# Eleven single-token lists interleaved with the last eleven two-list units of a PEER block

## The chip, the cores and the metric

The kernel runs on one core of a Trainium2 chip. Its engines are named as in the profile: PE (TensorE) multiplies matrices, DVE (VectorE) and ACT (ScalarE) work elementwise, POOL (GpSimd) issues the gathers, SP issues the plain transfers. The metric is the device time of one execution in microseconds; the time of a version is the median of its runs.

## The reference, cut to what matters

The kernel computes one decoder layer for 256 tokens of width 2048: a mixer (attention beside a state-space scan), and then a PEER feed-forward block, in which each token picks 16 experts in each of 8 heads out of 16384. An expert is one row of `expert_down` and one of `expert_up`. The change touches the PEER block alone:

```python
def peer_ffn(hn, w_query, sub_keys, expert_down, expert_up):
    ...                                   # product keys: the best 16 of 256 candidates per token and head
    gates = jax.nn.softmax(best_s, axis=-1)
    def block(args):
        xb, idx, gb = args
        u = expert_down[idx]
        act = jax.nn.gelu(jnp.einsum('thkd,td->thk', u, xb), approximate=False)
        vv = expert_up[idx]
        return jnp.einsum('thk,thkd->td', (gb * act).astype(vv.dtype), vv)
```

## The kernel before, in words

The mixer, the queries and the routing come first. Then the kernel sorts the used experts into lists of up to 128, one expert per partition. A gather fetches the rows of one list, 128 x 2048 floats, by an indirect DMA that POOL issues (`pump`, L1346). 17 further lists belong to experts whose lower products were computed densely and stored in `zd_dram`; they need no lower row.

*Lower products.* There are three kinds of lists. The 20 lists of kind C serve any token. The 44 lists of the two-list units (`unit_t`, L1460) serve only tokens of one half; a unit takes two such lists. In eight steps PE turns pieces of both rows (`tp`, L1475), ACT and DVE split them into a high and a low part (`turned`, L1449), and PE multiplies them by the tokens into `z` (L1488 to L1490); after the last step come GELU on ACT and a turning back (`zT`, L1504). The 30 single-token lists (`unit_d`, L1601) hold experts used by one token each. For such a list the kernel fetches its gates (`d_prep`, L1558), DVE finds in them the token of each expert (`find`, L1569 to L1571), PE turns the resulting one-hot matrix (`otb`, L1576), ACT copies it (`ot`, L1577), and then in four steps PE multiplies it by the tokens of h (`xe`, L1608) and DVE multiplies the gathered row by that with a running sum (L1614). The single-token lists need h turned (`turn_hn`, L1632): 64 transposes, copied by ACT into `hnt` in the buffers b2 and b3.

*Gates.* `gates` (L1240) builds a table of gates for all experts and tokens in the buffers b0 to b3 and stores each half in eight pieces to `g_dram` (`put`, L1262, on SP). `form` (L1688) fetches the gates of a list from `g_dram` (`fetch_gate`, L1431, on POOL) and multiplies them onto its products on DVE (`multiply`). It keeps a pace, a fraction of a list per step (FR).

*Upper products.* `up_load` and `up_go` (L1811, L1871) split a list's upper rows on ACT and DVE and multiply them by the gated products into `out` (L1889). The first 29 upper lists run among the single-token lists; 15 of them need no split. The others follow.

*What sets the order.* All of this is a list of items, each with a load part and a multiply part. `stream` runs them in order and emits the load parts up to LOOKT = 3 (or LOOKD = 2) items ahead. Work in `bg` (gates, turning h, forming) and in `due` advances by a step after each item. A scheduler then places the instructions of each engine, and every engine works through its own in order. The gathers form one queue in the order of `gathers`: one is issued when a slot of the `ring` is free (`release`, L1365). The ring has five slots during the lists C and the first units, four in the buffer `lo` and one in `xa`. When all gates are stored, `more_rows` (L1369) adds four more in b2 and b3 for the next units (up to unit 17, LATE); after them those buffers take the turned h. When the single-token lists begin (`begin`, L1588), the buffer of h becomes four more slots.

Of the kernel before, what the change touches and what calls it, by code (L numbers as in the profile page):

```python
# [18 lines left out]
P = 128  # L19
T = 256  # L20
# [79 lines left out]
TF = 8  # L100
TG = 4
XZ = 8
SBW = 10
SBR = 8
NPG = 2
# [3 lines left out]
FR = (0.27, 0.1, 0.35)  # L109
# [5 lines left out]
LATE = 17  # L115
TD = -8
# [27 lines left out]
def tile_block(ctx: ExitStack, tc: tile.TileContext, xT, w_f, w_v, w_dt, w_o, w_q, sk, dnt, down, up,  # L144
# [1095 lines left out]
    def gates():  # L1240
# [11 lines left out]
        def products(t0, B, A):  # L1252
            gp = ps_at(f"g_{t0}", (P, G2T, NK))
            for k in range(G2T):
                for j in range(2):
                    nc.tensor.matmul(gp[:, k, :], B[:, :, k], A[:, j, :, k], start=(j == 0), stop=(j == 1))  # L1256
            o = t0 % P
            for c in range(4):
                nc.scalar.activation(gbuf[c][:, :, o:o + G2T].rearrange("p i t -> p t i"), gp[:, :, 32 * c:32 * c + 32], AF.Copy)  # L1259
            if o == P - G2T:  # L1260
                h = t0 // P
                def put(c):  # L1262
                    cs = slice(16 * c, 16 * c + 16)
                    nc.sync.dma_start(g_dram[0:NE].rearrange("(i p) t -> p i t", p=P)[:, cs, h * P:(h + 1) * P],
                                        gbuf[c // 2][:, c % 2 * 16:c % 2 * 16 + 16, :])

                gens["put"] = [lambda c=c: put(c) for c in range(8)]
                gens["last"] = h
# [73 lines left out]
    def regions():  # L1342
        lo_t = rot("raws", "lo", 8192)
        ring.extend((lo_t[:, 2048 * k:2048 * (k + 1)], False) for k in range(4))

    def pump(most=99):  # L1346
        while most and pos[0] < len(gathers):
            what, j, late = gathers[pos[0]]
            can = [s_ for s_ in ring if not (late and s_[1])]
            if not can:  # L1350
                return
            ring.remove(can[0])
            where[what, j] = can[0]
            pos[0] += 1
            most -= 1
            with tc.issue_after(marks["pool"]) if what == "down" and "pool" in marks else ExitStack():
                g = nc.gpsimd.indirect_dma_start(out=can[0][0], out_offset=None, in_=down_rows if what == "down" else up_rows,  # L1357
                                                 in_offset=bass.IndirectOffsetOnAxis(ap=idx[:, 0, j:j + 1], axis=0))
            if "form" in gens and not stage[0]:
                marks["pool"] = g.ins  # L1360

    def row(what, j):
        return where[what, j][0]
# [5 lines left out]
    def more_rows():  # L1369
        while not gens.get("last") or gens["put"]:  # L1370
            yield
        yield from rest(SBW)
        for t in ("b2", "b3"):
            v = rot(f"rows_{t}", t, 4096)
            for k in range(2):
                ring.append((v[:, 2048 * k:2048 * (k + 1)], True))
                pump(1)
                yield from rest(SBR)
        gens["rows"] = True
# [41 lines left out]
    def hnt(p):  # L1421
        gated(0)
        return held(f"hnt{p}", f"b{p + 2}", F32R)
# [25 lines left out]
    def turned(tp, name, mark=False):  # L1449
# [6 lines left out]
        if mark and "form" in gens:  # L1456
            marks["act"], marks["dve"] = a, d
        return hi, lo

    def unit_t(k, r):  # L1460
# [20 lines left out]
        def go(hi, lo, s):  # L1481
            if s == 0:
                keep["z"] = ps_ms(f"z{j}")
            z = keep["z"]
# [6 lines left out]
            if s % 2 and last_b.get((k, r)) is not None:  # L1491
                gated(4)
# [4 lines left out]
            if s == 7:  # L1497
# [3 lines left out]
                def back():  # L1501
                    zT = ps_ms(f"zT{j}")
# [19 lines left out]
    def unit_c(r):  # L1522
# [11 lines left out]
        def go(hi, lo, s):  # L1534
            if s == 0 and r == 0:
                part["xa"] = rot("xa2", "xa", 4096)
                ring.append((part["xa"][:, 0:2048], False))
# [20 lines left out]
    def d_prep(n):  # L1558
# [15 lines left out]
        def turn_():  # L1574
            ot = gens["otb"][:, n % 4 * P:(n % 4 + 1) * P] if "otb" in gens else ps_ms(f"ot{n}", (P, P))
# [8 lines left out]
    def xbank():  # L1584
        gens["xb"].append(gens["xb"].pop(0))
        return gens["xb"][-1]

    def begin():  # L1588
# [6 lines left out]
        marks.pop("pool", None)  # L1595
        gens["x3"] = st.tile([P, 1024], F32R, tag="raw", bufs=NRAW, name="x3")
        v = rot("rows_hn", "hn", 8192)
        ring.extend((v[:, 2048 * k:2048 * (k + 1)], False) for k in range(4))
# [33 lines left out]
    def turn_hn():  # L1632
        while any(v[1] for v in where.values()) or pos[0] < late_at:
            yield
        ring[:] = [v for v in ring if not v[1]]
        for p in range(2):
            for tt in range(2):
                for c in range(4):
                    tp = ps_ms(f"hnt{p}{tt}{c}", (P, 512))
# [48 lines left out]
    def form():  # L1688
        while not gens.get("rows"):
            yield  # L1690
# [17 lines left out]
    for _, k, r in cs_:  # L1708
        items.extend(unit_c(r))
        gathers.append(("down", BASE[k] + r, False))  # L1710
    t_mark = len(items)
    for i, (_, k, r) in enumerate(ts_):
# [192 lines left out]
    def finish(tt, dc):  # L1905
# [5 lines left out]
    timed = [((n + 0.5) / len(ds_) + c / 1000, it, ("down", BASE[k] + r, False) if c == 0 else None)  # L1911
             for n, (_, k, r) in enumerate(ds_) for c, it in enumerate(unit_d(k, r))]
    timed += [((n + 1.0) / early + 0.002 * hf, ups[2 * n + hf], ("up", order[n], False) if hf == 0 else None)
# [7 lines left out]
    for n, _ in pieces[2 * early:]:  # L1921
        if n not in seen:
            seen.add(n)
            gathers.append(("up", order[n], False))
# [122 lines left out]
    bg.append(more_rows())  # L2047
# [14 lines left out]
    for n in range(DLOOK):  # L2062
        d_prep(n)
    stream(items, d_mark, d_mark)
# [91 lines left out]
```

## Time and profile before

| | |
|---|---|
| median of 3 runs | 1660.89 us (1660.86 to 1662.54) |
| the profiled execution | 1660.09 us |
| its span, first to last instruction | 1658.2 us |
| PE, DVE, ACT, POOL busy | 96%, 70%, 47%, 32% |
| mean granted clock of PE | 0.992 |
| two-list units, in the trace | 927.5 to 1172.3 us |
| single-token lists with the early upper lists | 1172.3 to 1356.0 us |
| the other upper lists, to the end | 1356.0 to 1658.2 us |

A row of a timeline has the start, the duration, the engine, the line of the kernel, the operation with its tiles, and in brackets how long the engine had been idle and what ended that. A row of a group has its count after x, then the busy time, the mean duration in ns of one, and the idle time before. PE's matmuls overlap, so a PE that is shown busy may still be slow; the number of matmuls in a stretch tells more. A table of stretches gives for each engine the busy time and the number of instructions, then the granted clock, the share of time in which the DMA engines were busy, and the rate.

### The profile page before, as it was taken

What the parts mean: (1) busy time and instruction counts of PE and PEld (TensorE: products, weight loads), DVE (VectorE), ACT (ScalarE), POOL (GpSimd) and SP (SyncE); (2) the same over time, 40 slices, a digit from 0 to 9 for tenths busy, and PEclk for the clock granted to TensorE, in tenths of its full rate; (3) what the DMA queues carried; (4) which work ended last, traced back from release to release, by engine and by line L of the source; (5) the groups of instructions that cost most, each with busy time, mean ns of one, the idle gap of its engine ahead of it and who ended that gap; (6) DMA issues with size and microseconds to landing.
All of it is one profiled execution on the core that took longest, in us unless ns stands there. A gap on an engine that the chain in (4) does not pass through costs nothing. (4 is left out here: it accounts for less than half of the span.)

```text
span 1658.2 us, 27347 instructions
## 1 busy us (share of the span) xinstructions
PE 1589.6 (96%) x10330; PEld 1404.5 (85%) x10331; DVE 1162.9 (70%) x2556; ACT 781.0 (47%) x1374; POOL 525.2 (32%) x499
## 2 busy tenths in 40 slices
PE   6999999999999999999999997999988999999997
PEld 6999979999888888899999996999755458887776
DVE  7776665853597988646646763655887667888886
ACT  5554457753111202335535664676431025667664
POOL 3001101121000000124414412424665655676851
PEclk9999999999999999999999998999999999999999
DMA  6655544667645433443392298745899999998893
GB/s 203 185 168 153 153 153 140 195 214 231 210 142 160 145 97 99 142 154 103 126 332 97 85 335 301 267 146 181 350 411 338 350 386 340 340 343 297 331 324 120
DMA packets 108809, 366.70 MB, mean 221 GB/s; under 512 B 12705, under 2 KB 48801, under 8 KB 82305
## 3 DMA queue, kind: packets, MB, share of 16 engines
q0 software_dynamic: 35504, 229.43, 37.4%
q1 hardware_dynamic: 70304, 134.23, 26.6%
q8 instruction: 83, 1.36, 0.3%
q10 hardware_dynamic: 2864, 1.24, 0.3%
q14 instruction: 54, 0.43, 0.1%
HBM read 337.24 MB, written 27.92 MB: 220 GB/s over the span
## 5 line engine op out<-in xcount | busy, mean ns | idle before, releaser
L1889 PE MATMUL out<-hi_up,p 128*128 128x512 f32 x716 | 193.7, 391 | 1.3 <-ACT hi_up L1822 1.3
L1455 DVE TENSOR_TENSOR t<-tp,t 128x512 fp32r<-128x512 f32 x176 | 120.9, 691 | 92.7 <-ACT t L1454 91.8
L1889 PEld LDWEIGHTS out<-hi_up,p 128*128 128x128 f32 x716 | 133.5, 188 | 31.3 <-ACT hi_up L1822 3.6
L253 PE MATMUL dn<-xt_t,raw_dn 128*128 128x256 f32 x640 | 158.3, 383 | 0.1
L1357 POOL DMA_INDIRECT raws<-in_down,idx x59 | 62.6, 1061 | 292.7 <-DVE colt L1196 161.8
L1432 POOL DMA_INDIRECT raw_small<-g_dram,idx x111 | 118.2, 1065 | 93.3 <-issue 45.0
L1454 ACT ACTIVATE t<-tp 128x512 fp32r<-128x512 f32 x176 | 105.4, 601 | 64.2 <-PE tp L1475 62.4
L253 PEld LDWEIGHTS dn<-xt_t,raw_dn 128*128 128x128 f32 x640 | 115.2, 193 | 11.7 <-issue 0.5
L253 PE MATMUL pq<-hg,raw_pq 128*128 128x256 f32 x512 | 112.9, 379 | 0.0
L253 PEld LDWEIGHTS pq<-hg,raw_pq 128*128 128x128 f32 x512 | 96.3, 190 | 12.6
L1259 ACT ACTIVATE big<-g 128x128 f32<-128x128 f32 x256 | 70.7, 437 | 75.8 <-PE g L1256 75.8
L1248 POOL TENSOR_TENSOR B<-B,gi 128x512 bf16<-128x512 bf16 x64 | 69.7, 1091 | 91.0 <-DVE B L1246 86.4
L1546 PE MATMUL zc<-hnl,c 128*128 128x256 f32 x320 | 95.9, 300 | 0.0
L1822 ACT ACTIVATE hi_up<-raws 128x1024 fp32r<-128x1024 f32 x74 | 76.7, 1057 | 31.8 <-PE out L1889 30.9
L1475 PE MATMUL tp<-ident,raws 128*128 128x128 f32 x464 | 90.4, 274 | 0.0
L1548 PE MATMUL zc<-hnl,c 128*128 128x256 f32 x320 | 89.1, 279 | 0.0
L1547 PE MATMUL zc<-hnl,c 128*128 128x256 f32 x320 | 89.0, 278 | 0.0
L1822 ACT ACTIVATE hi_up<-rows_hn 128x1024 fp32r<-128x1024 f32 x70 | 73.2, 1056 | 29.1 <-PE out L1889 26.2
L1455 DVE TENSOR_TENSOR c<-tc,c 128x512 fp32r<-128x512 f32 x80 | 55.2, 691 | 43.3 <-ACT c L1454 42.9
L1249 DVE TENSOR_TENSOR A<-O,gi 128x1024 f16<-128x1024 bf16 x64 | 47.5, 743 | 51.6 <-PE g L1256 51.3
L1608 PE MATMUL xe<-hnt,ot 128*128 128x512 f32 x240 | 78.3, 453 | 4.3 <-ACT ot L1577 3.4
L1889 PE MATMUL out<-lo_up,p 128*128 128x512 f32 x254 | 77.4, 397 | 4.4 <-DVE lo_up L1823 4.3
(539 smaller groups left out, 4654.4 us busy)
## 6 DMA issues: line engine op xcount, KB each, us to landing
raw_dn<-in_dnt SPq DMA_DIRECT2D x40, 512.0 KB, 3.9
raw_kq<-in_w_f SPq DMA_DIRECT2D x32, 512.0 KB, 3.8
raw_wo<-in_w_o SPq DMA_DIRECT2D x32, 512.0 KB, 4.7
raw_pq<-in_w_q SPq DMA_DIRECT2D x32, 512.0 KB, 3.8
g_dram<-big SPq DMA_DIRECT2D x16, 1024.0 KB, 13.9
raw_xb<-in_w_f SPq DMA_DIRECT2D x22, 512.0 KB, 4.4
raw_v<-in_w_v SPq DMA_DIRECT2D x16, 512.0 KB, 3.6
raw_z<-in_w_f SPq DMA_DIRECT2D x16, 512.0 KB, 4.0
```

The source lines that it names most:

```text
L253: nc.tensor.matmul(acc, raw[:, j * P:(j + 1) * P], mv[:, k * 8 + j, :], start=(k + j == 0), stop=(k * 8 + j == ND - 1))
L1259: nc.scalar.activation(gbuf[c][:, :, o:o + G2T].rearrange("p i t -> p t i"), gp[:, :, 32 * c:32 * c + 32], AF.Copy)
L1432: nc.gpsimd.indirect_dma_start(out=dst, out_offset=None, in_=g_half if w == P else g_dram, in_offset=bass.IndirectOffsetOnAxis(ap=idx[:, 1 ...
L1454: a = nc.scalar.activation(hi, tp, AF.Copy).ins
L1455: d = nc.vector.tensor_tensor(lo, tp, hi.bitcast(F32), op=OP.subtract).ins
L1475: nc.tensor.transpose(tp[:, (2 * dd + i) * P:(2 * dd + i + 1) * P], row("down", j + i)[:, d * P:(d + 1) * P], ident)
L1546: nc.tensor.matmul(z, wh, ah[:, d, :], start=(d == 0), stop=False)
L1547: nc.tensor.matmul(z, wh, al[:, d, :], start=False, stop=False)
L1548: nc.tensor.matmul(z, wl, ah[:, d, :], start=False, stop=(d == ND - 1))
L1608: nc.tensor.matmul(xe, gens[f"ot{n}"], hnt(p)[:, 2048 * k + 512 * c:2048 * k + 512 * (c + 1)], start=(p == 0), stop=(p == 1))
L1822: marks["act"] = nc.scalar.activation(hi, raw, AF.Copy).ins
L1889: nc.tensor.matmul(oa[tt][2 * hf + c], w[:, k * P:(k + 1) * P], mv[:, c * 512:(c + 1) * 512], start=(i == starts[f, tt, hf] and mv is hi a ...
```

## The change

- Eleven of the 30 single-token lists (DN) leave the stage with the early upper lists. The four steps of list n are put between the first four steps of two-list unit 11 + n (DU). Its row is gathered just before the rows of the next unit. Their `xe` uses the two PSUM banks of the tag `at` (named `xt`). The other 19 are spread over the same 29 upper lists.
- h is turned from unit 5 on (HU) instead of in units 16 to 18, and the first four single-token lists are prepared and `form` starts from unit 9 (GU) instead of unit 4. `form` has a pace of 0.2 instead of 0.27 at first.
- b2 and b3 hold the turned h from then on, so the ring keeps its five slots; `more_rows` is gone.
- The pieces of b2 and b3 are stored first of the second half, and the waits on the stores (`gated`) are set anew.
- The first ten plain units come before the buffered ones (TF, before eight). Sixteen instead of eight of the units' lists keep their products outside b0; the additional eight are in a 128 x 1024 tile `zr`, which is copied to b1 when the single-token stage begins.
- The units' `z` and `zT` share a bank, so that one is left for `otb`.

```diff
-TF = 8
-TG = 4
-XZ = 8
-SBW = 10
-SBR = 8
-NPG = 2
+TF = 10
+XZ = 16
+HU = 5
+GU = 9
+DU = 11
+DN = 11
+NPG = 4
...
-FR = (0.27, 0.1, 0.35)
+FR = (0.2, 0.1, 0.35)
...
-                gens["put"] = [lambda c=c: put(c) for c in range(8)]
+                gens["put"] = [lambda c=c: put(c) for c in (4, 5, 6, 7, 0, 1, 2, 3)]
...
-    def more_rows():
-        while not gens.get("last") or gens["put"]:
-            yield
-        yield from rest(SBW)
-        for t in ("b2", "b3"):
...
     def zh(n, w=P):
+        if n < 8:
+            return part["xa"][:, 3072 + P * n:3072 + P * n + w]
         if n < XZ:
-            return part["xa"][:, 3072 + P * n:3072 + P * n + w]
+            return part["zr"][:, P * (n - 8):P * (n - 8) + w]
         n -= XZ
         if n == 0:
-            gated(6)
+            gated(2)
...
     def hnt(p):
-        gated(0)
+        gated(6 - 2 * p)
...
             if s == 0:
-                keep["z"] = ps_ms(f"z{j}")
-            z = keep["z"]
+                if len(zbank) < DU:
+                    zbank.append(ps_ms(f"z{j}", (P, 512)))
+                else:
+                    zbank.append(zbank[-2])
+                keep["z"] = zbank[-1]
+            z = keep["z"][:, 0:T]
...
     def xbank():
+        if "xb" not in gens:
+            gens["xb"] = [ps_at(f"xt{k}", (P, 512)) for k in range(2)]
...
+    dus = [unit_d(k, r) for _, k, r in ds_]
     for i, (_, k, r) in enumerate(ts_):
-        items.extend(unit_t(k, r))
-        gathers += [("down", BASE[k] + r + x, i >= LATE) for x in range(2)]
-    late_at = SPC[LC] + 2 * LATE
+        u_mark.append(len(items))
+        u = unit_t(k, r)
+        n = i - DU
+        if 0 <= n < DN:
+            u = [x for p in zip(u[:4], dus[n]) for x in p] + u[4:]
+        items.extend(u)
+        if 0 <= n - 1 < DN:
+            gathers.append(("down", d_list[n - 1]))
+        gathers += [("down", BASE[k] + r + x) for x in range(2)]
...
-    stream(items, t_mark + 8 * TG)
+    part["zr"] = raw_tile("zr")
+    stream(items, u_mark[HU])
     pg_all = [t[:, T * k:T * (k + 1)] for t in [raw_tile(f"small{k}") for k in range(2)] for k in range(4)]
-    pgs.extend(pg_all[:NPG])
     gens["hnt"] = turn_hn()
-    gens["form"] = form()
-    bg.extend((gens["hnt"], gens["form"]))
-    stream(items, d_mark - 8)
+    bg.append(gens["hnt"])
+    stream(items, u_mark[GU])
     while gens["hnt"] in bg:
         work()
+    pgs.extend(pg_all[:NPG])
+    gens["form"] = form()
+    bg.append(gens["form"])
+    for n in range(DLOOK):
+        after(1 + 3 * n, lambda n=n: d_prep(n))
+    stream(items, d_mark, d_mark)
```

What this does to the order of the instructions shows at three places. The first is on POOL, where the first fetches of gates stand among the gathers of the units' rows (`raws` and `xa` are the ring's slots, `B` the last products of the table of gates). Before:

```order
L1357 DMA raws<-in_down,idx 128x2048 x2
L1248 TENSOR_TENSOR B_10213<-B_10213,gi 128x512
L1357 DMA raws<-in_down,idx 128x2048
L1357 DMA xa_7255<-in_down,idx 128x2048
L1357 DMA raws<-in_down,idx 128x2048 x4
L1432 DMA raw_small_10539<-g_dram,idx 128x128 x2
L1357 DMA xa_7255<-in_down,idx 128x2048
L1357 DMA raws<-in_down,idx 128x2048
```

After:

```order
L1355 DMA raws<-in_down,idx 128x2048 x2
L1248 TENSOR_TENSOR B_10213<-B_10213,gi 128x512
L1355 DMA raws<-in_down,idx 128x2048
L1355 DMA xa_7256<-in_down,idx 128x2048
L1355 DMA raws<-in_down,idx 128x2048 x4
L1355 DMA xa_7256<-in_down,idx 128x2048
L1355 DMA raws<-in_down,idx 128x2048 x4
L1355 DMA xa_7256<-in_down,idx 128x2048
L1355 DMA raws<-in_down,idx 128x2048 x2
L1420 DMA raw_small_10659<-g_dram,idx 128x128 x2
```

The fetches of gates, which read what SP stores to `g_dram`, have moved behind eight more gathers, the rows of four units.

The second place is PE in a late unit, from its second step on (`xt` are the list's products with h, `otb` the turning for a later list). After the change it reads so; before, the rows of `otb` and `xt` were not there:

```order
L1572 MATMUL otb<-ident,raw_small_10659 128x128
L1465 MATMUL tp_2_12693<-ident,raws 128x128 x4
L1609 MATMUL xt_11482<-hnt_10681,ot_12118 128x512
L1609 MATMUL xt_11482<-hnt_10850,ot_12118 128x512
L1482 MATMUL z_11248<-t_1_12671,hnl 128x256
...
L1498 MATMUL z_11388<-ident,zt_12680 128x128 x2
L1465 MATMUL tp_3_12715<-ident,raws 128x128 x4
L1609 MATMUL xt_11483<-hnt_10681,ot_12118 128x512
L1609 MATMUL xt_11483<-hnt_10850,ot_12118 128x512
```

Eight matmuls of 128x512 and a transpose of each list now stand between the unit's steps, on two banks in turn.

The third place is DVE in such a unit (`t` are the units' low parts, the rows of L1615 the list's four products):

```order
L1443 TENSOR_TENSOR t_0_12213<-tp_0_12208,t_0_12213 128x512
L1615 SCALAR_TENSOR_TENSOR raws,dsc<-raws,xt_11482 128x512
L1443 TENSOR_TENSOR t_1_12237<-tp_1_12232,t_1_12237 128x512
L1680 TENSOR_TENSOR zc<-zc,raw_small_10659 128x256
L1615 SCALAR_TENSOR_TENSOR raws,dsc<-raws,xt_11483 128x512
L1615 SCALAR_TENSOR_TENSOR raws,dsc<-raws,xt_11482 128x512
L1443 TENSOR_TENSOR t_2_12267<-tp_2_12262,t_2_12267 128x512
L1615 SCALAR_TENSOR_TENSOR raws,dsc<-raws,xt_11483 128x512
L1443 TENSOR_TENSOR t_3_12288<-tp_3_12283,t_3_12288 128x512
```

The four products stand among the first four low parts; a low part waits on DVE behind a product that waits for the list's row or for PE.

More of the change, by code (lines that the diff above doesn't have):

```diff
@@ L114 @@
 NA = 4
-LATE = 17
-TD = -8
+TD = -3
 HY = 1
@@ L1343, in regions @@
         lo_t = rot("raws", "lo", 8192)
-        ring.extend((lo_t[:, 2048 * k:2048 * (k + 1)], False) for k in range(4))
+        ring.extend(lo_t[:, 2048 * k:2048 * (k + 1)] for k in range(4))
     def pump(most=99):
         while most and pos[0] < len(gathers):
-            what, j, late = gathers[pos[0]]
-            can = [s_ for s_ in ring if not (late and s_[1])]
-            if not can:
+            what, j = gathers[pos[0]]
+            if not ring:
                 return
-            ring.remove(can[0])
-            where[what, j] = can[0]
+            where[what, j] = ring.pop(0)
             pos[0] += 1
@@ L1356, in pump @@
             with tc.issue_after(marks["pool"]) if what == "down" and "pool" in marks else ExitStack():
-                g = nc.gpsimd.indirect_dma_start(out=can[0][0], out_offset=None, in_=down_rows if what == "down" else up_rows,
+                g = nc.gpsimd.indirect_dma_start(out=where[what, j], out_offset=None, in_=down_rows if what == "down" else up_rows,
                                                  in_offset=bass.IndirectOffsetOnAxis(ap=idx[:, 0, j:j + 1], axis=0))
-            if "form" in gens and not stage[0]:
+            if "hnt" in gens and not stage[0]:
                 marks["pool"] = g.ins
     def row(what, j):
-        return where[what, j][0]
+        return where[what, j]
     def release(what, j):
@@ L1455, in turned @@
         d = nc.vector.tensor_tensor(lo, tp, hi.bitcast(F32), op=OP.subtract).ins
-        if mark and "form" in gens:
+        if mark and "hnt" in gens:
             marks["act"], marks["dve"] = a, d
         return hi, lo
+    zbank = []
     def unit_t(k, r):
@@ L1536, in go @@
                 part["xa"] = rot("xa2", "xa", 4096)
-                ring.append((part["xa"][:, 0:2048], False))
+                ring.append(part["xa"][:, 0:2048])
                 pump()
@@ L1574, in turn_ @@
         def turn_():
-            ot = gens["otb"][:, n % 4 * P:(n % 4 + 1) * P] if "otb" in gens else ps_ms(f"ot{n}", (P, P))
+            if "otb" not in gens:
+                gens["otb"] = ps_ms("otb", (P, 512))
+            ot = gens["otb"][:, n % 4 * P:(n % 4 + 1) * P]
             nc.tensor.transpose(ot, pg[:, P:T], ident)
@@ L1595, in begin @@
         marks.pop("pool", None)
+        kept = held("zh2", "b1")[:, 3072:4096]
+        nc.scalar.activation(kept, part["zr"], AF.Copy)
+        part["zr"] = kept
         gens["x3"] = st.tile([P, 1024], F32R, tag="raw", bufs=NRAW, name="x3")
         v = rot("rows_hn", "hn", 8192)
-        ring.extend((v[:, 2048 * k:2048 * (k + 1)], False) for k in range(4))
+        ring.extend(v[:, 2048 * k:2048 * (k + 1)] for k in range(4))
         pump()
@@ L1688, in form @@
     def form():
-        while not gens.get("rows"):
-            yield
         done_ = 0
@@ L1923, in tile_block @@
             seen.add(n)
-            gathers.append(("up", order[n], False))
+            gathers.append(("up", order[n]))
     def store(tt, dc):
```

30 lines of the change are left out of this document (10 added, 20 removed).

## The prediction

> **What bounds the kernel now.** I read the page, then a table of the stages (borders taken from PE's timeline), then the timelines where PE stops.
>
> ```profile
> PE 1589.6 (96%) x10330; PEld 1404.5 (85%) x10331; DVE 1162.9 (70%) x2556; ACT 781.0 (47%) x1374; POOL 525.2 (32%) x499
> ```
>
> ```profile
> core 0: us, PE busy (x) PEld busy (x) DVE busy (x) ACT busy (x) POOL busy (x), PEclk, DMA share, GB/s
> 927.50:986.56 59.06, 59.06 (x516) 58.43 (x514) 41.79 (x70) 39.27 (x103) 20.28 (x20) 1.00 0.65 220
> 986.56:1020.30 33.74, 21.37 (x167) 21.14 (x166) 11.14 (x17) 11.09 (x22) 7.55 (x8) 0.80 0.86 295
> 1020.30:1104.74 84.44, 84.44 (x741) 84.44 (x740) 51.84 (x84) 61.11 (x115) 29.72 (x32) 1.00 0.66 238
> 1104.74:1172.30 67.56, 63.36 (x543) 62.37 (x541) 36.32 (x70) 41.08 (x76) 26.24 (x28) 0.98 0.53 187
> 1172.30:1266.60 94.30, 81.67 (x308) 55.68 (x309) 83.73 (x233) 34.11 (x60) 64.05 (x57) 0.96 0.98 390
> 1266.60:1356.00 89.40, 83.71 (x253) 44.55 (x253) 55.66 (x212) 6.65 (x24) 50.14 (x53) 1.00 0.95 357
> 1356.00:1592.60 236.60, 232.47 (x1047) 190.22 (x1046) 195.67 (x274) 156.65 (x203) 162.13 (x134) 1.00 0.90 336
> ```
>
> PE looks full everywhere, but only three of these stretches are PE's own. Up to 1172.30 run the 22 two-list units; the third row holds nine of them (units 7 to 15) without a stop, 84.44 / 9 = 9.38 us each, with a third of the DMA time unused. The second row holds units 5 and 6 and took 33.74. From 1172.30 to 1356.00 the 30 single-token lists run among 29 early upper lists: 183.7 us in which PE starts 3.1 matmuls per us, against 4.4 in the next row, while DMA is busy 0.98 and 0.95. After 1356.00 PE is the bound (232.47 of 236.60). So two places can give time: units 5 and 6, and the single-token stage.
>
> Units 5 and 6, on POOL, on SP (the gate stores) and on PE:
>
> ```profile
> 983.62 0.94 POOL L1357 DMA_INDIRECT raws<-in_down,idx  x1 [0.30 <-PE tp L1475]
> 1006.03 0.95 POOL L1432 DMA_INDIRECT raw_small<-g_dram,idx  x1 [21.47 <-issue]
> 1008.54 0.95 POOL L1357 DMA_INDIRECT xa<-in_down,idx  x1 [0.30 <-issue]
> 960.19 38.99 SPq L1264 DMA_DIRECT2D g_dram<-big  x8
> 1014.14 0.48 PE L1475 MATMUL tp<-ident,xa 128*128 128x128 f32 x1 [12.37 <-DMA xa<-in_down,idx]
> ```
>
> POOL issues nothing for 21.47 us. The page says "issue", but the next instruction is the first fetch of gates, which can only start when the eight stores to g_dram, issued by SP from 960.19 to 999.18, have landed. The gather of the next unit's row stands behind it, and PE stops 12.37 us for that row.
>
> The single-token stage, one list's turn (list 8 to list 9):
>
> ```profile
> 1220.89 2.25 PE L1608 MATMUL xe<-hnt,ot 128*128 128x512 f32 x8 [0.46 <-ACT ot L1577]
> 1221.66 0.69 DVE L1614 SCALAR_TENSOR_TENSOR rows_hn<-rows_hn,xe 128x512 f32<-128x512 f32 x1 [0.66 <-PE xe L1608]
> 1224.10 1.22 DVE L1823 TENSOR_TENSOR lo_up<-rows_hn,hi_up 128x1024 fp32r<-128x1024 f32 x1
> 1225.23 1.22 DVE L1823 TENSOR_TENSOR x<-rows_hn,hi_up 128x1024 fp32r<-128x1024 f32 x1
> 1226.37 0.22 DVE L1569 TENSOR_SCALAR raw_small<-raw_small 128x128 f32<-128x128 f32 x1
> 1227.08 0.27 PE L1576 MATMUL otb<-ident,raw_small 128*128 128x128 f32 x1
> 1227.39 0.28 ACT L1577 ACTIVATE ot<-otb 128x128 fp32r<-128x128 f32 x1 [4.65 <-PE otb L1576]
> 1227.72 1.66 PE L1608 MATMUL xe<-hnt,ot 128*128 128x512 f32 x6 [0.37 <-ACT ot L1577]
> ```
>
> From one list's products (1220.89) to the next's (1227.72) are 6.83 us: four products on DVE, two subtractions for an upper list (2.44), the next list's find, its turning on PE, ACT's copy. A chain through DVE and PE, over a DMA that is full as well.
>
> **The change part by part.**
>
> The gate fetch. The first gate fetches now stand behind the gathers of four more units; released about a unit (9.38) apart, those carry POOL past 1020 before it meets the wait, and the stores had landed by 1006.03. The stop goes: 33.74 - 2 x 9.38 = **-15.0 us**. That is more than the 12.37, since PE restarts at a granted clock that makes the window's mean 0.80. [...]
>
> The late stops of the units. 1104.74:1172.30 holds 67.56 - 63.36 = 4.2 us of idle PE, around the finds of the first single-token lists. Those finds now lie within the later units, so I remove **-4.2** and charge stops there below.
>
> Eleven lists inside units 11 to 21. PE gets eight 128x512 matmuls and a transpose for each.
>
> ```profile
> 1593.80 44.75 PE out L1889 x196
> L1614 DVE SCALAR_TENSOR_TENSOR rows_hn<-rows_hn,xe 128x512 f32<-128x512 f32 x48 | 31.1, 683 | 14.0 <-PE xe L1608 13.9
> L1614 DVE DVE_READ_ACCUMULATOR rows_hn<-rows_hn,xe 128x1 f32 x48 | 3.9, 82 | 0.0
> L1455 DVE TENSOR_TENSOR t<-tp,t 128x512 fp32r<-128x512 f32 x73 | 50.0, 691 | 33.0 <-ACT t L1454 32.6
> L1571 DVE SCALAR_TENSOR_TENSOR raw_small<-raw_small,iota 128x128 f32<-128x128 f32 x26 | 7.5, 289 | 0.5
> L1570 DVE TENSOR_REDUCE dsc<-raw_small 128x1 f32<-128x128 f32 x26 | 7.2, 278 | 0.0
> L1675 DVE TENSOR_TENSOR xa<-xa,raw_small 128x128 f32<-128x128 f32 x6 | 1.7, 285 | 1.1 <-DMA raw_small<-g_dram,idx 1.0
> raws<-in_down,idx POOLq DMA_INDIRECT x9, 5.6
> rows_b<-in_down,idx POOLq DMA_INDIRECT x5, 7.7
> ```
>
> Back to back a 128x512 matmul costs 44.75 / 196 = 0.228 (the chain's row), so eight are 1.83; the row at 1220.89, with the tail of the last, says 2.25. With the transpose that is 2.1 to 2.5; I take 2.2, nearer the lower end, as other matmuls follow at once: 11 x 2.2 = **+24.2 us**. Nothing hides it, as PE has no gap in that stretch.
>
> DVE must keep up: 8 x 0.69 for a unit, 4 x (0.68 + 0.08) for a list, 0.9 for its find (0.22 + 0.28 + 0.29 and an accumulator read), some 0.7 for two or three gate products of 0.285 (27 of them now lie in the units, 22 before), 10.2 us in a unit of 9.38 + 2.2 = 11.6. It fits with 1.4 to spare, but the four products lie bunched: the third waits for matmuls just issued, and the subtraction of the next tile, which PE wants about 1.6 us later, stands behind it on DVE. I charge 0.6 us a unit; bounds 0 (DVE's slack takes it) and 2.0 (each of two bunches costs a subtraction and a product, 1.4, and some row comes late): **+6.6 us**.
>
> The ring of five rows. At a time two units' rows and one single-token row fill it, so the next single-token row is asked for when the previous list's last product frees its slot. From there to the point where PE wants the next list's first bank back are 11.6 less some 2.7 (an item of the unit, two of the list's matmuls, one product), so 8.9 us. A row lands 5.6 us after issue alone, 7.7 behind another (medians of 1020 to 1104.74), plus up to 0.95 for a POOL instruction in progress: 6.6 to 8.7. It just fits; no price beyond the 0.6.
>
> The single-token stage, now 19 lists among the same 29 upper ones. Two floors.
>
> ```profile
> GB/s 203 185 168 153 153 153 140 195 214 231 210 142 160 145 97 99 142 154 103 126 332 97 85 335 301 267 146 181 350 411 338 350 386 340 340 343 297 331 324 120
> ```
>
> Transfers: 94.30 x 390 + 89.40 x 357 = 68.7 MB; eleven rows of 128 x 2048 x 4 bytes and their gate fetches take away 12.3; 56.4 MB last 145 us at 390 GB/s and 151 at the stage's mean of 374. Chain: a list costs 6.83 - 2.44 = 4.4, so 183.7 - 11 x 4.4 = 135. Transfers decide: 148, so **-36 us**. Bounds: -46 (at 411 GB/s, the page's best slice and one of this stage, 137 us) and -26 (158 us, at the 357 GB/s of the stage's second half).
>
> ```profile
> L1822 ACT ACTIVATE hi_up<-raws 128x1024 fp32r<-128x1024 f32 x74 | 76.7, 1057 | 31.8 <-PE out L1889 30.9
> 960.19 13.34 SPq L1264 DMA_DIRECT2D g_dram<-big  x4
> ```
>
> At nothing: turning h, moved from units 16 to 18 to 5 and 6, the same 64 transposes either way; its copies wait on ACT only for the stores of their own buffers, which now are the first four, issued by 973.53, while unit 5 begins at 986.56. The last gate products: the upper stage gets 68 multiply instructions instead of 69. One added ACT copy of 128x1024, 1.06 us by the row of that size, lies at the units' end, where ACT is busy for 41.08 of 67.56 us.
>
> Sum against the profiled execution (1660.09, span 1658.2): -15.0 - 4.2 + 24.2 + 6.6 - 36 = -24.4, so 1635.7; the median shown is 0.8 higher: **1636**.
>
> **The rivals.**
>
> A. *Lists cost their chain in the units too.* If find, turning, products run as serially as at 1220.89, each costs 4.4 instead of 2.8: +17.6, 1654. For it: the same four products, DVE at 88%. Against: in the new order the turning stands four lists ahead.
>
> B. *Slower: single-token rows come late.* If the two rows of the next unit get ahead of it (1.05 MB each, 2.7 us at 390 GB/s), a row lands 12 to 14 us after its slot is free, 3 to 5 us late; DVE waits in front of the next subtraction, PE behind it. From 0.6 + 24.4 / 11 = 2.8 us a unit the change loses; at 4.5 it is 1636 + 3.9 x 11 = 1679. For it: five rows instead of nine, POOL in order. Against: that gather stands ahead of the unit's two on POOL. [...]
>
> C. *The gain is given back.* The upper stage has DMA at 0.90; if it starts with an empty ring of nine rows, PE waits up to 9 x 2.7 = 24 us: 1660. Against: the ring also refills during the stage before, in which the last lists need few transfers.
>
> D. *The change does not remove the wait, it moves it.* ACT's copies into b2 and b3 wait for stores too. If the fourth store lands late, ACT stops and the units with it, at worst by the old 15: 1651. Against: the 13 us between its issue and unit 5.
>
> **How the numbers follow.** Forecast 0.72, A 0.12, B 0.07, C 0.05, D 0.04. With its terms at their ends the forecast reaches from 1636 - 6.6 - 10 - 1 = 1618 (no stop in the units, 137 us for the stage, 2.1 a list on PE) to 1636 + 15.4 + 10 + 3 = 1664; all three at the upper end is unlikely, and 1656 leaves out the last of it. 1618 to 1656 takes in A and D and leaves out B, C and the forecast's tail, under 2 in 10. About 0.2% is what can be told from no change. Faster by more: the forecast, D and nearly all of A, 0.87; within: C, 0.05; slower: B and tails, 0.08.
>
> **What would show it.** Right: no POOL gap of 20 us before the first gate fetch and units 5 and 6 near 26 us with the turning in them; units 11 to 21 at 11.6 to 12.5 us each, with PE idle under 1 us in each; the units' end near 1183 and the single-token stage near 148 us with DMA still over 0.9. Wrong: PE stops of 2 us or more in each late unit, released by DVE whose products wait for a row (B) or for PE (A); the single-token stage above 160; a stop at 1330 to 1360 as the upper stage begins (C); ACT copies to hnt waiting for DMA near 990 (D).

## The result, and the profile after

| | before | after |
|---|---|---|
| median | 1660.97 us (1660.86 to 1662.54, 4 runs) | 1633.11 us (1630.61 to 1635.78, 4 runs) |
| ratio | 1 | 0.9829, 95% interval 0.9816 to 0.9843 |
| span of the profiled execution | 1658.2 us | 1628.7 us |
| first two-list unit to last | 244.8 us | 253.1 us |
| single-token lists, to the last product | 181.2 us | 145.1 us |
| the rest, to the end | 304.8 us | 302.7 us |

The change is faster by 28 us, 1.7%; forecast were 1636, in a range of 1618 to 1656. The units became 8.3 us longer, the single-token stage 36.1 shorter, and the rest 2.1 shorter: 29.5 us of span. Two of the runs below hold one execution each at a granted clock of 0.70 or 0.75 (2101.69 and 1953.54 us), which their ratios leave out.

The first rows of the page of the changed kernel, and its table of stretches (units 0 to 4, 5 to 7, 8 to 10, 11 to 21; the single-token stage in two parts; the upper stage in two):

```profile
PE 1580.7 (97%) x10330; PEld 1402.2 (86%) x10331; DVE 1156.0 (71%) x2556; ACT 779.5 (48%) x1375; POOL 531.1 (33%) x499
```

```profile
927.81:986.84 59.03, 59.03 (x516) 58.43 (x514) 41.76 (x70) 39.30 (x103) 20.24 (x20) 1.00 0.64 220
986.84:1021.91 35.07, 35.07 (x313) 35.07 (x312) 16.60 (x25) 24.33 (x48) 5.63 (x6) 1.00 0.90 313
1021.91:1050.20 28.29, 28.29 (x247) 28.15 (x246) 17.29 (x36) 19.88 (x40) 14.12 (x15) 1.00 0.62 222
1050.20:1180.89 130.69, 125.25 (x994) 119.36 (x993) 98.23 (x254) 72.49 (x142) 69.98 (x75) 1.00 0.79 291
1180.89:1252.30 71.41, 63.14 (x259) 46.97 (x258) 65.24 (x165) 31.93 (x53) 50.62 (x43) 0.98 1.00 404
1252.30:1328.00 75.70, 72.02 (x202) 35.94 (x200) 35.64 (x136) 5.75 (x17) 38.27 (x41) 1.00 0.96 369
1328.00:1563.00 235.00, 233.00 (x1047) 189.80 (x1046) 194.07 (x273) 154.90 (x202) 169.50 (x133) 1.00 0.89 335
1563.00:1628.70 65.70, 56.24 (x243) 45.12 (x242) 49.01 (x53) 36.29 (x44) 19.33 (x14) 0.96 0.54 188
```

In the second row PE is busy for all of its 35.07 us at full clock: the stop of 12.37 us is gone, and the 6.9 us beyond three times 9.38 go to the 64 transposes of h (313 matmuls, where three units had 248). In the fourth row PE is busy for 125.25 of 130.69 us, so it is close to being the bound of the units with a list in them. In the fifth and sixth DMA is busy for all or nearly all of the time, as it was before.

POOL around its first gate fetch, in the timeline of the changed kernel:

```profile
1027.10 0.94 POOL L1355 DMA_INDIRECT raws<-in_down,idx  x1 [7.19 <-PE tp L1465]
1029.59 0.95 POOL L1420 DMA_INDIRECT raw_small<-g_dram,idx  x1 [0.30 <-issue]
```

It comes at 1029.59, without a wait, where before POOL waited 21.47 us. What still stops PE in units 11 to 21 is shown by the table of waits, whose numbers are the us in total, the times and the longest:

```profile
PE tp L1465 <- DVE t L1443: 3.2, 4, 1.8
PE z L1483 <- DVE t L1443: 2.3, 1, 2.3
```

The longest of these stops, with the row of DVE that stands ahead of it:

```profile
1057.36 0.29 DVE L1673 TENSOR_TENSOR xa<-xa,raw_small 128x128 f32<-128x128 f32 x1 [3.48 <-DMA raw_small<-g_dram,idx]
1058.31 0.38 PE L1483 MATMUL z<-t,hb 128*128 128x256 f32 x1 [2.28 <-DVE t L1443]
```

DVE is about to multiply gates onto a list's products and stands 3.48 us for their fetch; the low part `t` that PE wants comes next on DVE. The stops of 1.83 us at 1154.77 and of 0.74 us at 1072.06 follow in the same way on waits of 2.24 and 1.14 us for a fetch of gates. These three are 4.85 of the 5.44 us.

### The profile page after: what moved, and what is told of

The parts are those of the page before. It is cut to its first block, busy times and chain, and to the rows that moved or that the text cites. A ratio compares the mean times of both kernels' runs of the same rounds, so it can differ in the third digit from the quotient of the medians.

```text
span 1628.7 us, 27340 instructions
## 1 busy us (share of the span) xinstructions
PE 1580.7 (97%) x10330; PEld 1402.2 (86%) x10331; DVE 1156.0 (71%) x2556; ACT 779.5 (48%) x1375; POOL 531.1 (33%) x499
## 3 DMA queue, kind: packets, MB, share of 16 engines
q8 instruction: 83, 1.36, 0.3%
## 5 line engine op out<-in xcount | busy, mean ns | idle before, releaser
L1355 POOL DMA_INDIRECT raws<-in_down,idx x71 | 72.3, 1018 | 303.8 <-DVE colt L1196 161.9
L1420 POOL DMA_INDIRECT raw_small<-g_dram,idx x111 | 123.5, 1113 | 43.5 <-issue 28.7
L253 PEld LDWEIGHTS pq<-hg,raw_pq 128*128 128x128 f32 x512 | 96.3, 190 | 12.5
L1465 PE MATMUL tp<-ident,raws 128*128 128x128 f32 x544 | 95.5, 273 | 2.2 <-DVE t L1443 2.2
L1829 DVE TENSOR_TENSOR lo_up<-rows_hn,hi_up 128x1024 fp32r<-128x1024 f32 x58 | 71.2, 1234 | 13.3 <-ACT hi_up L1828 10.5
L1355 POOL DMA_INDIRECT rows_hn<-in_up,idx x48 | 63.0, 1312 | 46.7 <-DVE lo_up L1829 12.9
```

Source lines behind the costliest of these rows:

```text
L253: nc.tensor.matmul(acc, raw[:, j * P:(j + 1) * P], mv[:, k * 8 + j, :], start=(k + j == 0), stop=(k * 8 + j == ND - 1))
L1355: g = nc.gpsimd.indirect_dma_start(out=where[what, j], out_offset=None, in_=down_rows if what == "down" else up_rows, in_offset=bass.Indir ...
L1420: nc.gpsimd.indirect_dma_start(out=dst, out_offset=None, in_=g_half if w == P else g_dram, in_offset=bass.IndirectOffsetOnAxis(ap=idx[:, 1 ...
L1465: nc.tensor.transpose(tp[:, (2 * dd + i) * P:(2 * dd + i + 1) * P], row("down", j + i)[:, d * P:(d + 1) * P], ident)
L1829: marks["dve"] = nc.vector.tensor_tensor(lo, raw, hi.bitcast(F32), op=OP.subtract).ins
```

## The experiments: where the 15 us at the gate stores were

The theory: the first gate fetch waits on POOL for the gate stores, gathers queue behind it, and PE stops; moving the fetch behind the gathers of some more units is worth 15 us. The rival: the stores are what is waited for, and whoever comes first stops.

**Forming from unit 9 in the kernel before.**

```diff
     gens["hnt"] = turn_hn()
+    bg.append(gens["hnt"])
+    stream(items, t_mark + 8 * 9)
     gens["form"] = form()
-    bg.extend((gens["hnt"], gens["form"]))
+    bg.append(gens["form"])
```

> The kernel before, with forming started at unit 9 in place of unit 4 and nothing else. Theory: the wait of POOL for the gate stores, and PE's stop of 12 us with the slower clock behind it, is gone: 1661 less 15 is 1646 (1643 to 1650), units 5 and 6 near 19 us. Rival (gate products started later are missing later, in the upper lists): 1655 or more.

Measured 1662.21 us (1660.85 to 1664.65), ratio 1.000 (0.999 to 1.0009): nothing was won. ACT, POOL and PE in its trace:

```profile
988.91 0.63 ACT L1419 ACTIVATE hb<-hnl 128x512 fp32r<-128x512 f32 x1 [13.73 <-DMA g_dram<-big]
995.64 0.94 POOL L1357 DMA_INDIRECT rows_b<-in_down,idx  x1 [18.75 <-ACT hb L1419]
990.81 1.12 PE L1475 MATMUL tp<-ident,raws 128*128 128x128 f32 x4 [12.12 <-DVE t L1455]
```

The stop is there with 12.12 us instead of 12.37, in unit 3 where it was in unit 6 (an expectation below calls this one unit earlier), and begins on another engine. ACT's copy of the tokens of h into `hb` goes into b1, which the stores still read. In the kernel before this copy has its place after a mark that is set once `form` exists; my edit created `form` later, and so the copy moved ahead to 975 (in the trace of before it runs at 1022). ACT works in order, so the splitting of the units' rows stood behind it for 13.73 us; the copy began at 988.91, 0.1 us after the second store of b1 had landed. The edit was not the clean one that I took it for, and it shows that the wait does not belong to the fetch.

**The fetch alone later** (the kernel before, the fetch tied behind the last gather; the copy to `hb` stays in place):

```diff
     def fetch_gate(dst, j, w):
-        nc.gpsimd.indirect_dma_start(out=dst, ...
+        with tc.issue_after(marks["pool"]) if "pool" in marks else ExitStack():
+            nc.gpsimd.indirect_dma_start(out=dst, ...
```

> The kernel before, with the first gate fetch held behind some ten more gathers, the late rows among them, which stay where they were; with the late rows moved too it took 1645.9. Theory: the late rows go into buffers that the gate stores hold, so POOL's wait passes to the first of them and only part of the 15 us goes: 1650 to 1659. Rival: the fetch alone made the stop, and the late rows find their stores landed: 1644 to 1648.

Measured 1658.28 us (1652.60 to 1663.20), ratio 0.9939 (0.9919 to 0.9959). The kernel before took 1670.43 on that chip, so the ratio counts: 1650.8 on the scale of the others, if that chip lengthens both kernels alike. POOL and PE in the timeline, then the stretches of units 5 and 6 and of unit 7:

```profile
1002.67 0.94 POOL L1357 DMA_INDIRECT rows_b<-in_down,idx  x1 [11.56 <-ACT t L1455]
1010.45 0.33 PE L1476 MATMUL tp<-ident,rows_b 128*128 128x128 f32 x1 [2.13 <-DMA rows_b<-in_down,idx]
```

```profile
983.54:1002.28 18.74, 18.74 (x167) 18.74 (x165) 11.08 (x17) 11.16 (x21) 1.88 (x2) 1.00 1.06 364
1002.28:1014.00 11.72, 9.59 (x84) 9.36 (x83) 5.53 (x9) 8.41 (x17) 6.57 (x7) 1.00 1.02 366
```

Units 5 and 6 run through. POOL now stands for 11.56 us at the first late row (`rows_b`), which goes into b2, a buffer that the stores read too. PE feels 2.13 us of it, in unit 7. The row names ACT as the releaser. But the second store of b2, issued at 981.73, took 20.2 us to land, at 1001.9, and the gather follows 0.8 us later, as the first gate fetch of the kernel before follows the last store (landed at 1005.1, fetch at 1006.03). So the late row waits for its buffer.

**Fetch and late rows later**, the copy to `hb` in place:

```diff
-SBW = 10
+SBW = 26
```

with the tied fetch above.

> The kernel before, with the late rows (into the last two buffers) two units later and the first gate fetch held behind them, nothing else. In the run with forming from unit 9 the stop came back one unit earlier, on ScalarE's copy to hb, because that edit also freed that copy from its place. Here the copy keeps the place that it had before. Theory: the 15 us of units 5 and 6 belong to whoever stands first for the buffers that the gate stores still hold; with all three users (fetch, late rows, copy) behind the stores' landing, units 5 and 6 take about 18.8 us and the time is 1645 to 1649. Rival 1: the wait only finds a fourth user: 1658 to 1663. Rival 2: the stop goes, but the gates formed two units later cost it back as stops in units 16 to 21: 1654 to 1662.

Measured 1645.90 us (1643.81 to 1646.89), ratio 0.9906 (0.9886 to 0.9927), as the theory had it. The stretches of units 5 and 6, of units 16 to 21 and of the single-token stage up to its last product in this run, and then the last of these in the kernel before:

```profile
984.57:1003.30 18.73, 18.73 (x167) 18.73 (x165) 11.06 (x17) 11.16 (x21) 3.75 (x4) 1.00 1.06 360
1087.71:1150.34 62.63, 62.13 (x544) 61.72 (x542) 36.41 (x65) 41.24 (x76) 26.95 (x28) 1.00 0.51 183
1150.34:1336.79 186.45, 163.71 (x555) 100.24 (x556) 140.10 (x445) 40.07 (x83) 113.53 (x110) 0.97 0.95 364
```

```profile
1172.29:1353.45 181.16, 162.83 (x555) 99.44 (x556) 138.48 (x440) 40.55 (x83) 112.23 (x108) 0.98 0.97 374
```

33.74 us became 18.73: exactly the 15.0 of the prediction, by order alone and with nothing of the change beside it. A side result: PE's 4.2 us of late stops went too (idle now 62.63 - 62.13 = 0.5), but the single-token stage became 5.3 us longer. Most of this is one kind of stop that has moved. The longest late stop in the kernel before, with the row of DVE ahead of it and the first find behind it:

```profile
1168.17 0.29 DVE L1675 TENSOR_TENSOR zh<-zh,raw_small 128x128 f32<-128x128 f32 x1 [4.03 <-DMA raw_small<-g_dram,idx]
1169.12 0.39 PE L1489 MATMUL z<-t,hnl 128*128 128x256 f32 x1 [2.33 <-DVE t L1455]
1170.71 0.35 DVE L1569 TENSOR_SCALAR raw_small<-raw_small 128x128 f32<-128x128 f32 x1
```

In this run, in the single-token stage:

```profile
1159.47 0.29 DVE L1676 TENSOR_TENSOR zh<-zh,raw_small 128x128 f32<-128x128 f32 x1 [3.82 <-DMA raw_small<-g_dram,idx]
1160.02 0.80 PE L1890 MATMUL out<-hi_up,p 128*128 128x512 f32 x1 [3.58 <-DVE p L1792]
```

In the kernel before, DVE waits 4.03 us for a fetch of gates ahead of this stop, and 3.47 us ahead of the other one (1.42 us at 1157.56). The finds, to which the prediction put these stops, come after both. In this run such a wait, of 3.82 us, lies 9 us inside the next stage and stops PE for 3.58 us there.

**Forming from unit 5 in the changed kernel**

```diff
-GU = 9
+GU = 5
```

> The changed kernel with GU = 5: forming starts with the turning of h at unit 5, so that the first two gate fetches stand on POOL where they stood before the change. Theory: POOL waits for the last store, PE stops again, 1633 + 15 is 1648 (1645 to 1651). Rival (the new order of the stores or the other changes removed the wait): 1631 to 1637.

Measured 1637.25 us, ratio 0.9851 (0.9831 to 0.9871): 4 us over the changed kernel and not 15, at the edge of the rival's range, though the rival's reason, a wait that is gone, is not what happened. POOL, ACT and PE in the timeline, then the stretches of units 5 to 7 and 11 to 21:

```profile
1006.95 0.95 POOL L1420 DMA_INDIRECT raw_small<-g_dram,idx  x1 [21.25 <-issue]
997.08 1.09 ACT L1643 ACTIVATE hnt<-hnt 128x512 fp32r<-128x512 f32 x2 [3.84 <-issue]
997.73 1.97 PE L1641 MATMUL hnt<-ident,hnl 128*128 128x128 f32 x8 [3.55 <-ACT hnt L1643]
```

```profile
987.52:1032.59 45.07, 40.01 (x316) 38.30 (x315) 18.97 (x44) 26.14 (x51) 13.82 (x15) 0.92 0.77 256
1060.72:1186.78 126.06, 124.58 (x992) 119.28 (x992) 97.81 (x247) 71.88 (x139) 68.01 (x72) 1.00 0.81 299
```

POOL's wait is back in full, 21.25 us, but the stretch is only 10.0 longer than 35.07: the transposes of h need no row and run while POOL stands, so PE idles for only 5.06 us (45.07 - 40.01) and loses most of the rest to a clock of 0.92. Its longest stop there, 3.55 us, is for ACT's copies of turned h, which come sooner in this run and stood 3.84 us; they go on at 997.08, when the store issued at 974.82 has just landed (22.2 us later). This is the wait of rival D, in small. And 4.6 us come back in units 11 to 21 (126.06 against 130.69, PE idle 1.48 against 5.44), where the gates are formed earlier.

**Forming from unit 7** follows from that:

```diff
-GU = 9
+GU = 7
```

> The changed kernel with forming from unit 7 in place of 9. With forming from unit 5 PE's idle time in units 11 to 21 was 1.5 us, against 5.4 with 9, but units 5 to 7 took 45.07 us against 35.07, since the fetch stood in front of the stores' landing (1007). From 7 the fetch stands behind three more gathers. Theory: the fetch comes at or after the landing, so units 5 to 7 stay at 35 to 36 us, and the stops of units 11 to 21 shrink by 2 to 4: 1628 to 1631. If the fetch still waits: 1635 to 1638. If the stops in units 11 to 21 do not hang on the gates: 1632 to 1634.

Measured 1629.01 us (1626.51 to 1630.36), ratio 0.9805 (0.9785 to 0.9825), within the theory's 1628 to 1631. POOL's first gate fetch, then units 5 to 7, 8 to 10 and 11 to 21, and all that stops PE in the last:

```profile
1012.00 0.95 POOL L1420 DMA_INDIRECT raw_small<-g_dram,idx  x1 [2.86 <-issue]
```

```profile
987.00:1022.10 35.10, 35.10 (x313) 35.10 (x311) 17.15 (x29) 24.32 (x47) 11.41 (x13) 1.00 0.91 309
1022.10:1052.00 29.90, 29.09 (x249) 28.51 (x248) 18.59 (x42) 20.28 (x42) 14.34 (x16) 1.00 0.66 249
1052.00:1178.40 126.40, 125.04 (x992) 119.34 (x992) 97.87 (x248) 71.87 (x140) 67.64 (x71) 1.00 0.81 298
```

```profile
PE tp L1465 <- DVE t L1443: 0.9, 2, 0.6
PE z L1483 <- DVE t L1443: 0.3, 1, 0.3
```

POOL waits 2.86 us for the last store (issued at 995.96, landed 15.1 us later), so the fetch does stand a little ahead of the landing; but PE does not stop in units 5 to 7. The stops of units 11 to 21 go from 5.44 to 1.36 us, and DVE's waits for fetches of gates there from 10.0 to 3.1. So most of the 0.5 us a unit that these stops cost in the changed kernel, and that I had charged to crowded products on DVE, was late forming. Units 8 to 10 take back 1.6 us (29.90 against 28.29). The medians are 4 us apart, the spans 1628.7 and 1624.7; as the intervals of the ratios overlap, that this version beats the changed kernel is likely, not settled.

## The experiments: the ring of five

**The unit's rows ahead of the single-token row**, in the changed kernel's queue of gathers:

```diff
+        gathers += [("down", BASE[k] + r + x) for x in range(2)]
         if 0 <= n - 1 < DN:
             gathers.append(("down", d_list[n - 1]))
-        gathers += [("down", BASE[k] + r + x) for x in range(2)]
```

> The changed kernel with one exchange in the queue of gathers: the single-token row is asked for behind the two rows of the next unit, not ahead of them. Theory (a ring of five leaves 8.9 us for this row, and it just fits): the row comes 3 to 4 us late in each of eleven units, 1633 + 33 to 44 is 1666 to 1677, with PE stops behind DVE products that wait for the row. Rival (the row has slack): 1631 to 1640.

Measured 1684.37 us (1680.55 to 1684.75), ratio 1.0135 (1.0118 to 1.0152): 51 us over the changed kernel, slower than before it, and 7 us above the theory's range. Units 11 to 21, what PE waits for in them, and what DVE waits for in the products of single-token rows:

```profile
1049.05:1222.85 173.80, 143.61 (x991) 128.60 (x991) 96.19 (x244) 70.16 (x142) 65.47 (x69) 0.93 0.56 205
```

```profile
PE tp L1465 <- DMA raws<-in_down,idx: 14.5, 11, 2.2
PE tp L1465 <- DMA xa<-in_down,idx: 5.5, 3, 3.5
PE xt L1609 <- DVE raws L1615: 4.5, 3, 3.8
DVE raws L1615 <- DMA raws<-in_down,idx: 6.8, 3, 5.1
DVE xa L1615 <- DMA xa<-in_down,idx: 1.3, 1, 1.3
```

43 us more in these eleven units, 3.9 each: that is the price of rival B, whose mechanism this is, made to happen; 7 more lie in the single-token stage (154.15 us from 1222.85 to 1377.00, against 147.11 from 1180.89 to 1328.00). B had DVE and PE wait behind a late single-token row; DVE does, by 8.1 us in all and 5.1 at the longest, but 20.0 us of PE's waits are for the units' own rows. That these are asked for late because each slot is held longer by a late single-token row is an argument, not a reading. The order of three gathers decides between 1.7% won and 1.4% lost.

## The experiments: transfers or chain in the single-token stage

**Half rows.** The 19 lists of the stage fetch 1024 of 2048 numbers per row, and two of their four products use them again.

```diff
+    down_halves = down.rearrange("a b (h d) -> (a b h) d", h=2)
...
+                half = what == "down" and j in d_list[DN:]
+                g = nc.gpsimd.indirect_dma_start(out=where[what, j][:, 0:1024] if half else where[what, j], ...
...
+            cc = c if n < DN else c % 2
```

> The changed kernel, with only half of each row (1024 of 2048 numbers, from another place) gathered for the 19 lists of the single-token stage, and the third and fourth product using the half again; so half of these rows is left out and the products are of other numbers, while every instruction of PE, DVE and ACT stays. It takes 19 x 0.52 = 10 MB of 57 MB from the stage's transfers, about 25 us at the stage's 390 to 404 GB/s. Theory (the stage is bounded by its transfers, 145 to 151 us, with the chain of a list just below at 135): -8 to -14 us, 1619 to 1626. If the chain alone decides: 1631 to 1635. If the transfers alone decide and no chain follows: 1606 to 1611.

Measured 1624.40 us (1622.05 to 1628.25), ratio 0.9778 (0.9753 to 0.9804).

**Narrow products.** Three of the four products of each of these lists have 64 instead of 512 columns.

```diff
+            wd = 512 if n < DN or c == 0 else 64
```

> The changed kernel, with three of the four products of each of the 19 lists in the stage cut from 512 to 64 columns, so that part of these products is left out; transfers stay. The chain of a list becomes about 3 x 0.5 = 1.5 us shorter, 19 x 1.5 = 29 us in all. Theory (transfers decide): 0 to -4 us, 1629 to 1634. Rival (the chain decides): 1603 to 1612.

Measured 1628.30 us (1625.02 to 1632.23), ratio 0.9806 (0.9783 to 0.9829), 0.7 us below the theory's range and far from the rival's. The stage from the last unit to the last product in the changed kernel, with half rows, and with narrow products:

```profile
1180.89:1326.00 145.11, 133.16 (x454) 81.97 (x453) 99.94 (x296) 36.13 (x67) 87.47 (x82) 0.99 0.98 388
```

```profile
1186.45:1318.77 132.32, 127.47 (x454) 81.94 (x453) 101.26 (x296) 37.81 (x68) 88.84 (x82) 1.00 0.92 344
```

```profile
1180.35:1319.72 139.37, 130.45 (x452) 82.89 (x451) 76.15 (x295) 35.96 (x67) 82.93 (x82) 0.99 1.00 402
```

10 MB less to transfer shorten the stage by 12.8 us of the 25 that they take, and end at 132: the prediction's floor for the chain was 135. 24 us less work on DVE (76.15 against 99.94) shorten it by 5.7, and then DMA is busy all the time at 402 GB/s. So transfers bound the stage, and something else holds it 13 us below. That this is the chain, as forecast, fits the 135, but is not shown: no run takes both away, and PE is shown busy for 127.47 of those 132.32 us. Beside the transfers the chain costs a little more than the nothing that I put down, because it still leaves DMA 2% idle and 14 GB/s short. With half rows the median fell by 8.7 and not 12.8, since units 11 to 21 took longer there. PE has stops of 2.19 and 2.81 us at 1059.24 and 1074.86, behind waits of DVE for gates of 3.38 and 3.21 us, where the changed kernel has 3.48 and 1.14; why the second fetch came later stays open.

## The experiments: a list inside a unit

**No lists in the units** (all 30 stay in the stage; the rest of the change as it is):

```diff
-DN = 11
+DN = 0
```

> The changed kernel with DN = 0: no single-token list among the units, all 30 with the early upper lists, everything else as changed. Theory (two separate gains: the gate fetch's wait, 15 us plus 4 of late stops, and the lists' move, 36 us less in the single-token stage against 24 on PE and some 6 of stops in the units): only the small gain of the move is lost, 1638 to 1643 us, the units' stage ends near 1150 and the single-token stage lasts 180 to 184. Rival (the lists' move is nearly all of the gain): 1655 to 1661.

Measured 1644.14 us, ratio 0.9892 (0.9876 to 0.9909), 1 us above the theory's range; of this kernel no trace is used, so that the forecasts for its stages stay unchecked. So moving the lists is worth some 11 us, give or take 3.5 by the two intervals, and the remainder of the change 17 to 18 (1 - 0.9892). The prediction's terms for the move are 36 - 24.2 - 6.6 = 5.2, so it had the gain of the move at about half its size.

**One part of h**: the eleven lists use only the high part of h, with four matmuls in place of eight.

```diff
-            for p in range(2):
+            ps_ = 1 if n < DN else 2
+            for p in range(ps_):
```

> The changed kernel, with the eleven lists inside the units multiplied by the high part of h alone (four matmuls of 512 columns in place of eight), so that the low part is left out there. It takes 11 x 4 = 44 matmuls from PE in units 11 to 21, 10.0 us at the 0.228 us each of the prediction. Theory (PE bounds these units, and a list costs there what PE works on it): 1622 to 1626. Rival (rows, finds or the copies bound these units, and PE waits for them anyway): 1630 to 1634.

Measured 1651.02 us (1645.53 to 1657.75) beside 1670.43 before, ratio 0.9880 (0.9846 to 0.9914): not faster than the changed kernel, rather slower, and far outside the theory's range. Units 11 to 21:

```profile
1056.60:1198.80 142.20, 127.87 (x951) 117.24 (x950) 95.94 (x242) 68.21 (x142) 66.44 (x72) 0.96 0.70 258
```

43 matmuls fewer than in the changed kernel, but 14.3 us of idle PE instead of 5.4 and a clock of 0.96. Taken alone this would say that PE is not what bounds these units. But it ran on a chip on which the kernel before took 0.6% longer, and unit 9, ahead of any list, took 14.1 us there against 9.4, from its first matmul into `z` to that of unit 10. Edit and chip cannot be told apart; the run leaves PE's price of a list open.

**Twelve and thirteen lists, forming from unit 7**, were run beside it, on the same chip:

```diff
-GU = 9
-DU = 11
-DN = 11
+GU = 7
+DU = 10
+DN = 12
```

> The changed kernel with forming from unit 7 and twelve lists in units 10 to 21. Eleven lists were worth 11 us against none (1644.1 to 1633.1), so a twelfth 1 us, on top of 1629.0 with forming from 7: 1627 to 1629. If the first list's gates come late in unit 10 or the ring of five runs dry there: 1630 to 1636.

Measured 1646.65 us (1644.66 to 1650.32), ratio 0.9861 (0.9831 to 0.9891).

> As the one with twelve, with thirteen lists in units 9 to 21: 1626 to 1629 if each list is worth 1 us; 1631 to 1640 if the lists come ahead of their gates (forming begins only two units earlier) and PE stops for them.

With DU = 9 and DN = 13: 1643.78 us (1640.59 to 1645.83), ratio 0.9844 (0.9812 to 0.9876). With the 1660.97 us of the kernel before, these ratios are 1638 and 1635 us, above the first ranges of both. Neither ratio is below the 0.9805 of eleven lists with forming from 7. From the first matmul into `z` of unit 11 to that of unit 21 a unit took 12.7 and 12.2 us in them, against 11.6 there, on the slower chip again. There is no sign that more lists help, and no proof that they harm.

## Why the prediction was right, by its steps

- *The gate fetch, -15.0.* Units 5 to 7 have no stop, and their 35.07 us are three units of 9.38 and 6.9 us of turning, where they were 43.11 us before (986.37 to 1029.48). As the 6.9 are found by the same 9.38, this is no measurement of its own; the run with late rows and fetch is one: by itself, in the kernel before, the order is worth 15.0 in these units. The 2.6 us beyond the stop are PE at a lower clock after it: in the trace of before the granted clock is 0.50 from PE's restart at 1014.14 to 1019, 0.81 from there to 1020 and 1.00 from then on; its mean from 1014.14 to 1020.30 is 0.57, and 6.16 x 0.43 = 2.6. But the reason was half of one. Fetch, late rows, the copy to `hb` and the copies of turned h all wait for the same stores, and the change wins because it deals with all four: the fetch is later, the late rows are gone, the copy to `hb` comes in unit 9 and not in unit 7 (from 1033, where the last store landed at 1010.4), and the pieces of b2 and b3, which take the turned h, are stored first. Had it moved the fetch alone, a wait would have been left.
- *Rival D, the wait moves to the copies of turned h*, did not happen: the first of these waits 0.55 us, for PE, and so do the others that wait (6.8 us in 14 waits). It shows when the turning runs faster, with forming from unit 5.

```profile
988.27 0.60 ACT L1643 ACTIVATE hnt<-hnt 128x512 fp32r<-128x512 f32 x1 [0.55 <-PE hnt L1641]
```

- *The late stops, -4.2*: this reading was wrong, and that the sum held in spite of it is luck. The stops were not at the finds but at products on DVE that wait for a fetch of gates (3.75 of the 4.2 us), and the changed kernel has 4.85 us of such stops, in other units.
- *Eleven lists on PE, +24.2*: 125.25 - 11 x 9.38 = 22.1, 2.0 each instead of 2.2. The eight matmuls of a list take 2.04 us up to the start of what follows (pairs of 0.46, 0.48, 0.55 and 0.55, from 1097.56 on); those at 1220.89 take 2.08 by that measure, up to 1222.97, and 2.25 with the tail.
- *Stops in these units, +6.6*: 130.69 - 125.25 = 5.4, 0.5 a unit. The size was nearly right and the cause was not: two stops behind fetches of gates make 4.1 of it, 2.28 us in unit 11 and 1.83 in unit 19, more than the 1 us that was given as a sign of being right. With forming from unit 7 the stops shrink to 1.4 in all, so DVE's bunched products cost little. That later forming delays the gates is a cost of the change that I put at nothing; it was some 4 us in these units. With the term before, forecast were -4.2 + 6.6 = +2.4, measured 5.4 - 4.2 = +1.2.
- *The units*: forecast -15.0 - 4.2 + 24.2 + 6.6 = +11.6, measured +8.3; most of the difference is PE's price of a list. Units 11 to 21 take 11.9 each, within 11.6 to 12.5, and end at 1180.9 (forecast 1183).
- *The ring of five*: it just fits: DVE waits for a single-token row five times, 5.3 us in all and 1.9 at the longest, and none of PE's three longest stops is behind these. With the queue in the other order it does not fit. Rival B was the dangerous one, and its 3.9 us a unit the right size.
- *The single-token stage, -36*: 181.16 - 145.11 = 36.05, the transfers as the bound shown by taking them away. 145.11 us at 388 GB/s are 56.3 MB, where 56.4 were forecast.
- *Rival C, an empty ring at the upper stage*: the rest took 302.7 us instead of 304.8, so nothing was given back. These 2 us are the one part of the gain that no step had, and a part that two executions may differ by.

The sum of the trace, +8.28 - 36.05 - 2.05 = -29.8, with 0.3 us by which the units begin later, is the 29.5 of the spans.

## What to carry to other kernels

When an instruction waits for a store at the head of an in-order queue, list every user of the buffers that the store reads before moving one of them: the next in line takes over the wait, here the late row on POOL with 11.56 us or the copy on ACT with 13.73. Work that needs neither the row nor the queue, here the turning of h, can cover part of what is left (10.0 us in place of 15). When an engine waits for another, read what that other one was waiting for just before: here it told the fetches of gates from the finds beside them. And where a ring has just enough slots, the order in which its slots are asked for counts: here it is the difference between 1633 and 1684 us.

## What was not expected of the hardware

The clock fell without a stop like the 12.37 us of the kernel before. In the run with the unit's rows first, PE's stops and the clock around them were:

```profile
1103.51 0.41 PE L1465 MATMUL tp<-ident,xa 128*128 128x128 f32 x2 [1.21 <-DMA xa<-in_down,idx]
1107.08 0.47 PE L1465 MATMUL tp<-ident,raws 128*128 128x128 f32 x1 [2.02 <-DMA raws<-in_down,idx]
```

```profile
1104.00:1106.00 2.00, 0.81 (x6) 0.34 (x4) 0.00 (x0) 0.39 (x1) 0.00 (x0) 1.00 0.98 352
1106.00:1108.00 2.00, 0.92 (x5) 0.92 (x6) 0.00 (x0) 0.00 (x0) 0.00 (x0) 0.70 0.98 408
1108.00:1110.00 2.00, 2.00 (x10) 1.78 (x10) 1.35 (x3) 1.94 (x5) 0.00 (x0) 0.50 0.32 129
```

Stops of 1.21 and 2.02 us, 3.6 us apart, and then a granted clock of 0.70 and of 0.50. Over these eleven units the clock averaged 0.93; PE's two longest stops there were 3.8 and 3.5 us, the others at most 2.2. In the changed kernel the clock stayed at 1.00 after the stop of 2.28 us (in each us from 1055 to 1062), so the length of the last stop does not tell the two cases apart; what does is not shown.

The same kernel took 1660.97 to 1662.03 us on some chips and 1670.43 on another, with a wider spread there (1665.02 to 1674.36; elsewhere 1659.95 to 1666.21 at the widest). Edits worth less than 1% that ran only there could not be placed beside the others.
